# Odd layer of a hybrid encoder: conv-tile transposes issued two tiles later, SSD factors issued one head pair earlier

## The chip, the cores and the metric

The kernel runs on one core of a Trainium2 chip. A core has a matrix engine (TensorE, PE in the profile; PEld is its weight load), a vector engine (VectorE, DVE), an activation engine (ScalarE, ACT), a general engine (GpSimd, POOL) and a queue that starts transfers (SyncE, SP). Each engine runs its own list of instructions in order and waits on semaphores for the others. The metric is the device time of one execution in microseconds.

## The reference

A bidirectional encoder trunk with a sequence of 512, a width of 1024 and two layers, in float32. The first (even) layer is attention beside a convolution module. The second (odd) layer, which the change touches, projects the normalized input to 6192 columns and feeds two mixers from them:

```
u = rms_norm(x, norm_g) @ w_in
z_c, xbc, dt_f, dt_b, g_b, g_c, h_d, z_d = split(u)
xbc = silu(dw_conv5(xbc) + conv_b)          # x: 1536 columns, B: 4 x 128, C: 4 x 128
y   = ssd_scan forward + ssd_scan backward + d_skip * x      # 24 heads of 64, 4 groups, chunks of 128
o_c = group_rms_norm(y * silu(z_c))
o_d = g_b * dw_conv3(g_c * h_d) * silu(z_d)
x   = x + concat(o_c, o_d) @ w_out
```

Inside a chunk the scan is a product with a masked, decayed matrix; between chunks a state of 128 x 64 per head is carried. The program ends with an rms norm.

## The kernel before, in words

All large products are done with operands split into a high and a low part (fp32r), three matmuls for each pair of blocks: high by high, high by low, low by high. Weights arrive by DMA as slabs of 128 x 1024 (`w_raw`, two buffers); ScalarE makes the high part (L87) and, in the odd layer's input projection, POOL the low part (L88). `Weights.next` prepares one slab ahead of the one in use.

The odd layer's input projection is cut into 40 entries (`odd_tiles`): four z entries that are token-major, and 36 channel tiles of 128 channels by 512 positions. A channel tile is 24 matmuls of 512 columns into one of three `acc` banks (`mm_cm`, L318). Tiles of kind C, B and x go through `conv5` (L707 to L716): ScalarE writes the centre tap into an SBUF page, VectorE adds four taps from the bank (L714), ScalarE takes a tanh (L715), VectorE completes the silu (L716). B and x tiles are then turned on TensorE with four 128 x 128 transposes into an `sb` bank (helper `transposed`, L266) and copied by ScalarE. Tiles h, gc, gb and zd of each of four channel blocks make the short convolution.

The SSD works on four groups of six heads. `ssd_prepare(g)` makes the masked products of C and B (`cbm`) and the six states that enter the chunks: VectorE scales x (L854), TensorE multiplies by the turned B (L856), ScalarE or POOL and VectorE carry the state on (L859 to L862). `ssd_pairs(g)` treats three pairs of heads. For each head it makes the factor f of 128 x 512: VectorE and ScalarE alternate over the four chunks (L892, L893 on f; L897, L898 on the decay e, which `decays` fetches by DMA two heads ahead into a ring of four buffers), then an exponential (L900) and a product (L901). Then come eight matmuls with f (L904, into the only `cv` bank), the skip term (L913), the part of the states (L920 on TensorE, L925 and L928 on VectorE) and the gate product on POOL (L930). After each pair, `fill` issues a few tiles of the rest of the list. `ssd_finish(g)` takes the group norm and turns the result (L944, L266 into `tp`), scaled into the pages that the output projection reads.

The order of the code sets priorities and the buffers' order. The framework plans each engine's list from it ahead of time and may put an instruction whose inputs it takes to be late behind later ones: in the trace the transposes of a tile stand within the matmuls of the following tile. On the chip each list is then fixed.

`fill` issues in group order 5, 9, 9 and 8 tiles, in threes or twos after a pair; before the first group nine entries are issued (z, and group 0's C, B and three x tiles).

Of the kernel before, what the change touches and what calls it, by code (L numbers as in the profile page):

```python
# [159 lines left out]
def odd_tiles():  # L160

    group = lambda g: [("C", g), ("B", g), ("x", 3 * g), ("x", 3 * g + 1), ("x", 3 * g + 2)]
    short = lambda i: [("h", i), ("gc", i), ("gb", i), ("zd", i)]
    z = [("z", g) for g in range(4)]
    return z + group(0) + group(1) + short(0) + group(2) + short(1) + group(3) + short(2) + short(3)


ODD_TILES = odd_tiles()
# [2 lines left out]
def trunk(ctx, tc, A, out, dbg=None):  # L171
# [29 lines left out]
    def bank(tag):  # L201
        return ps.tile([P, S], F32, name=tag, tag=tag, bufs=banks[tag])
# [504 lines left out]
    def conv5(key, i, c):  # L707

        z = mm_cm(key, xT)
        w = lambda j: pc[:, PC["conv_c_w"][0] + i * 5 + j:PC["conv_c_w"][0] + i * 5 + j + 1]  # L710
        d = tmp("c5t", "c5", 3)
        SC.activation(c, z, AF.Identity, scale=w(2), bias=pcs("conv_c_b", i))  # L712
        for j, o, ii in taps5:
            V.scalar_tensor_tensor(c[:, o], z[:, ii], w(j), c[:, o], op0=ALU.mult, op1=ALU.add)  # L714
        SC.activation(d, c, AF.Tanh, scale=0.5)  # L715
        V.scalar_tensor_tensor(c, d, 1.0, c, op0=ALU.add, op1=ALU.mult)  # L716
# [9 lines left out]
    def channel_tile(kind, i):  # L726
# [6 lines left out]
        elif kind == "C":  # L733
            inp[i]["C"] = tmp("CT", "CT", 2)
            conv5("C", 16 + i, inp[i]["C"])
            inp[i]["x"] = tmp("xs", "xs", 2, (P, NT, GW))
        elif kind == "B":
            bt = tmp("BT", "BT", 1)
            conv5("B", 12 + i, bt)
            tp = transposed([bt[:, t * P:(t + 1) * P] for t in range(NT)], "sb")  # L740
            inp[i]["B"], inp[i]["Bt"] = bt, tmp("Bt", "Bt", 1)
            SC.copy(inp[i]["Bt"], tp)
        elif kind == "x":
            c = tmp("c5", "c5", 3)
            conv5("x", i, c)
            tp = transposed([c[:, t * P:(t + 1) * P] for t in range(NT)], "sb")
            g, j = divmod(i, 3)
            SC.copy(inp[g]["x"][:, :, j * P:(j + 1) * P], c4(tp))
        elif kind == "h":
            sc["h"] = tmp("sc_h", "c5", 3)  # L750
            SC.copy(sc["h"], mm_cm("h", xT))
        elif kind == "gc":
            z, hp = mm_cm("gc", xT), sc["h"]
            V.tensor_tensor(hp, z, hp, op=ALU.mult)
            c = oF[i] = page("oF", "keep")
            SC.activation(c, hp, AF.Copy, scale=cdw[:, i, 1:2])
            for j, o, ii in taps3:
                V.scalar_tensor_tensor(c[:, o], hp[:, ii], cdw[:, i, j:j + 1], c[:, o], op0=ALU.mult, op1=ALU.add)  # L758
        elif kind == "gb":
            z = mm_cm("gb", xT)  # L760
            V.tensor_tensor(oF[i], z, oF[i], op=ALU.mult)
        else:
            z = mm_cm("zd", xT)
            gate(sc["h"], z)
            G.tensor_tensor(oF[i], oF[i], sc["h"], op=ALU.mult)

    todo = iter(ODD_TILES)

    def fill(n):
        for _ in range(n):  # L770
            kind_i = next(todo, None)
            if kind_i:
                channel_tile(*kind_i)

    fill(2)

# [19 lines left out]
    back = bank("tp")  # L796
    for d in range(2):
        tp = transposed([d1[:, t, d * SH:(d + 1) * SH] for t in range(NT)], "tp", SH)
        cs = tmp("cs", "c5", 3)[:SH]
        for c in range(NT):  # L800
            o, i, z = cs[:, c * P:(c + 1) * P], tp[:, c * P:(c + 1) * P], ident[:SH]
            if d:
# [70 lines left out]
            nc.sync.dma_start(e, src.broadcast_to([P, 2, S]))  # L873
            ahead.append(e)

    def ssd_pairs(g, cbm, St, fills):

        CT, xs = inp[g]["C"], inp[g]["x"]
        hs = heads(g)
        for j in range(3):  # L880
            pr = slice(j * P, (j + 1) * P)
            yd = bank("cv")
            for i in range(2):
                hh = g * HPG + 2 * j + i
                hf, hb = hh, SH + hh

                decays(hh + 2)
                rb = ahead[hh]
                e, f = rb[:, 0], tmp("f", "f", 3)
                for c in range(NT):  # L890
                    cc = slice(c * P, (c + 1) * P)
                    SC.activation(f[:, cc], cbm[0][:, cc], AF.Copy, scale=dt[:, c, hf:hf + 1])  # L892
# [6 lines left out]
                                           op0=ALU.add, op1=ALU.min)  # L899
                SC.activation(e, e, AF.Exp)  # L900
                V.tensor_tensor(f, e, f, op=ALU.mult)  # L901
                for c in range(NT):
                    o = c * P + i * HD
                    T.matmul(yd[:, o:o + HD], f[:, c * P:(c + 1) * P],  # L904
# [23 lines left out]
                V.tensor_tensor(yc, yc, yw.rearrange("p (c d) -> p c d", c=3), op=ALU.add)  # L928
            zj = zg[g][:, :, pr]
            G.tensor_tensor(yt, yt, zj, op=ALU.mult)  # L930
            fill(fills[j])

    def ssd_finish(g):

# [7 lines left out]
        rsqrt(rs, ss, 4)  # L942
        for c in range(NT):
            V.tensor_scalar(xs[:, c], xs[:, c], rs[:, c:c + 1], None, op0=ALU.mult)  # L944
        for j in range(3):
            i = 3 * g + j
            tp = transposed([xs[:, c, j * P:(j + 1) * P] for c in range(NT)])
# [1 line left out]
                oF[4 + i] = zg[g].rearrange("p c d -> p (c d)")[:, j * S:(j + 1) * S]  # L949
                SC.activation(oF[4 + i], tp, AF.Copy, scale=pcs("ssd_norm", i))  # L950
            else:
                hi, lo = tmp("o_hi", *(("c5", 3), ("c5", 3), ("CT", 2))[j], dt=F32R), \
                    tmp("o_lo", *(("c5", 3), ("BT", 1), ("CT", 2))[j], dt=F32R)
                split_psum(hi, lo, tp, pcs("ssd_norm", i))
                last.append((hi, lo))

    last = []
    fill(7)
    pre = ssd_prepare(0)
    for g in range(GRP):  # L960
        ssd_pairs(g, *pre, ((2, 2, 1), (3, 3, 3), (3, 3, 3), (3, 3, 2))[g])
        if g < GRP - 1:
            pre = ssd_prepare(g + 1)
        ssd_finish(g)


    free = []
# [118 lines left out]
```

## Time and profile before

| | us |
|---|---|
| median of 3 runs | 1000.29 |
| lowest, highest | 997.64, 1002.73 |
| the profiled execution | 1003.47 |
| its span, first to last instruction | 1001.7 |

The granted clock of TensorE is the share of full speed that the hardware allowed; its mean over the profiled execution is 0.978. The odd layer's first z matmul starts at 509 us, its first channel tile ends at 590 us, the last channel tile ends at about 901 us, and the output projection runs from there to the end. In the views below a row of a group gives line, engine, operation, output and inputs, shapes and count, then busy time and mean length, then the engine's idle time just before and what ended it; a row of the timeline gives start, length, engine, line, operation and, in brackets, the idle time before and who ended it; a row of the waits gives who waited for whom, total us, times and the longest.

### The profile page before, as it was taken

The page shows a single profiled execution, that of the slowest core. Times are in us where ns is not written, and L with a number is a line of the kernel's source. Part 1 is how long each engine was busy: PE and PEld are TensorE (multiplying, and loading weights), DVE is VectorE, ACT ScalarE, POOL GpSimd, SP SyncE. Part 2 cuts the span into 40 slices and gives each one's busy share as a digit, 9 for nine tenths or more (in the row PEclk, how much of TensorE's full clock was granted, in tenths as well). Part 3 has the DMA queues.
Part 4 walks back from the last instruction along what each step waited for, and adds up shares of the span by engine and source line. Part 5 has one row for each costly group of instructions (what it writes and reads, how often), then busy time and mean ns, then how long its engine had stood idle before and what let it go on. Part 6 is the DMA issues. An engine that isn't in the chain of part 4 may idle for free. (4 is left out here: it accounts for less than half of the span.)

```text
span 1001.7 us, 12583 instructions
## 1 busy us (share of the span) xinstructions
PE 931.6 (93%) x4564; PEld 757.0 (76%) x4564; DVE 735.9 (73%) x1295; ACT 464.5 (46%) x916; POOL 384.0 (38%) x272
## 2 busy tenths in 40 slices
PE   7899999999999999699999999888869988999996
PEld 7887686686786777578889987676756876787885
DVE  4799989899898998922167537888998968956215
ACT  6646444454445453723143546456455555443312
POOL 0251743625428153531234354424433433445221
PEclk9999999999999999989999999989999998999999
DMA  8313322112213235033253533332333423322222
GB/s 302 101 29 111 55 68 70 49 40 84 69 25 115 74 31 170 22 127 105 81 173 92 168 125 96 95 110 83 92 120 84 122 90 102 109 101 82 92 84 84
DMA packets 42326, 95.99 MB, mean 96 GB/s; under 512 B 12136, under 2 KB 13800, under 8 KB 42264
## 3 DMA queue, kind: packets, MB, share of 16 engines
q1 hardware_dynamic: 42264, 95.19, 31.2%
q8 instruction: 36, 0.59, 0.2%
q14 instruction: 26, 0.21, 0.1%
HBM read 90.85 MB, written 4.33 MB: 95 GB/s over the span
## 5 line engine op out<-in xcount | busy, mean ns | idle before, releaser
L88 POOL TENSOR_TENSOR w_lo<-w_raw,w_hi 128x1024 fp32r<-128x1024 f32 (+2 forms) x68 | 159.5, 2347 | 267.2 <-ACT w_hi L87 181.2
L87 ACT CAST w_hi<-w_raw 128x1024 fp32r<-128x1024 f32 (+7 forms) x142 | 135.1, 952 | 221.8 <-PE acc L318 67.1
L318 PE MATMUL acc<-xT_hi,w_hi 128*128 128x512 f32 x544 | 222.0, 409 | 2.7 <-ACT xT_hi L404 2.7
L318 PE MATMUL acc<-xT_lo,w_hi 128*128 128x512 f32 x544 | 220.4, 406 | 0.4 <-POOL xT_lo L405 0.4
L88 DVE TENSOR_TENSOR w_lo<-w_raw,w_hi 128x1024 fp32r<-128x1024 f32 (+6 forms) x74 | 85.3, 1153 | 116.1 <-ACT w_hi L87 111.8
L318 PE MATMUL acc<-xT_hi,w_lo 128*128 128x512 f32 x544 | 142.7, 396 | 0.0
L479 DVE SCALAR_TENSOR_TENSOR cv<-u,pc,cv 128x497 f32<-128x497 f32 (+10 forms) x176 | 130.2, 740 | 10.0 <-ACT cv L468 7.7
L318 PEld LDWEIGHTS acc<-xT_hi,w_hi 128*128 128x128 f32 x544 | 105.3, 194 | 25.5 <-ACT xT_hi L404 2.9
L318 PEld LDWEIGHTS acc<-xT_lo,w_hi 128*128 128x128 f32 x544 | 105.3, 194 | 22.5 <-POOL xT_lo L405 0.8
L318 PEld LDWEIGHTS acc<-xT_hi,w_lo 128*128 128x128 f32 x544 | 101.9, 189 | 20.8
L477 POOL TENSOR_TENSOR side<-side 128x510 f32<-128x510 f32 (+3 forms) x56 | 77.9, 1391 | 4.7
L482 POOL TENSOR_TENSOR u<-cs,side 128x512 f32<-128x512 f32 x8 | 11.0, 1372 | 157.1 <-issue 149.9
L898 DVE SCALAR_TENSOR_TENSOR e<-e,nacs 128x128 f32<-128x128 f32 x96 | 50.8, 571 | 7.1 <-ACT e L897 7.1
L531 ACT ACTIVATE p<-sb,mx 128x512 f32<-128x512 f32 x64 | 43.4, 683 | 20.9 <-DVE mx L529 20.6
L476 POOL TENSOR_SCALAR side<-u,pc 128x510 f32<-128x510 f32 (+3 forms) x56 | 50.9, 910 | 4.7
L529 DVE TENSOR_REDUCE mx<-sb 128x1 f32<-128x512 f32 x64 | 41.7, 685 | 3.3 <-PE sb L527 2.6
L893 DVE SCALAR_TENSOR_TENSOR f<-cbm,dt,f 128x128 f32<-128x128 f32 x96 | 42.5, 488 | 0.4 <-ACT f L892 0.4
L897 ACT ACTIVATE e<-e,nacs 128x128 f32<-128x128 f32 x96 | 31.3, 391 | 21.6 <-DMA e<-acs 21.6
L266 PEld LDWEIGHTS tp<-kc,p 128*128 128x128 f32 x256 | 28.9, 140 | 16.0 <-ACT pt L554 10.7
L714 DVE SCALAR_TENSOR_TENSOR c<-acc,pc,c 128x510 f32<-128x510 f32 (+1 forms) x48 | 35.7, 744 | 6.7 <-ACT c L712 6.4
L527 PE MATMUL sb<-k_t,qk_hi 128*128 128x512 f32 (+1 forms) x128 | 39.5, 403 | 0.4 <-DVE k_t L257 0.3
L564 PE MATMUL acc<-pt,v_tm 128*64 128x512 f32 x128 | 37.6, 608 | 1.4 <-DVE pt L554 1.4
(336 smaller groups left out, 1927.4 us busy)
## 6 DMA issues: line engine op xcount, KB each, us to landing
w_raw<-in_w_cm_o SPq DMA_DIRECT2D x36, 512.0 KB, 3.5
w_raw<-in_w_cm_e SPq DMA_DIRECT2D x32, 512.0 KB, 3.5
e<-acs SPq DMA_DIRECT2D x24, 512.0 KB, 5.2
w_raw<-in_w_out_e SPq DMA_DIRECT2D x16, 512.0 KB, 3.5
w_raw<-in_w_out_o SPq DMA_DIRECT2D x16, 512.0 KB, 3.5
w_raw<-in_w_z SPq DMA_DIRECT2D x12, 384.0 KB, 3.2
xt<-in_xT SPq DMA_DIRECT2D x8, 256.0 KB, 5.4
x_t<-in_x SPq DMA_DIRECT2D x4, 512.0 KB, 6.5
```

What stands on the lines that cost most here:

```text
L87: nc.scalar.copy(hi, raw)
L88: eng.tensor_tensor(lo, raw, hi.bitcast(F32), op=ALU.subtract)
L318: T.matmul(a, l, r, start=n == 0, stop=n == 3 * kk - 1)
L476: G.tensor_scalar(t[:, o], ut[:, i], wt(j), 0.0, op0=ALU.mult, op1=ALU.add)
L477: G.tensor_tensor(side[:, o], side[:, o], t[:, o], op=ALU.add)
L479: V.scalar_tensor_tensor(c[:, o], ut[:, i], wt(j), c[:, o], op0=ALU.mult, op1=ALU.add)
L527: T.matmul(s, l[:, qs], r, start=n == 0, stop=n == 2)
L529: V.tensor_reduce(mx, s, axis=AX.X, op=ALU.max, negate=True)
L531: SC.activation(p, s, AF.Exp, bias=mx, accum_out=sums[:, q:q + 1])
L564: T.matmul(o[j * HD:(j + 1) * HD], v_tm[:, k, (h0 + j) * HD:(h0 + j + 1) * HD], pt, start=k == 0, stop=k == NT - 1, skip_group_check=True)
L893: V.scalar_tensor_tensor(f[:, cc], cbm[1][:, cc], dt[:, c, hb:hb + 1], f[:, cc], op0=ALU.mult, op1=ALU.add)
L898: V.scalar_tensor_tensor(e[:, cc], rb[:, 1, cc], nacs[:, c, hb:hb + 1], e[:, cc], op0=ALU.add, op1=ALU.min)
```

## The change

Four edits that go together. First, the turning of a B or x tile becomes a closure that `fill` calls once two further tiles have been issued (`late=2`); `fill(0)` calls all that are left. Second, `ssd_pairs` is split into `ssd_factors` (the two factors f of a pair) and `ssd_pair` (all that reads them); the factors of the next pair are issued before the matmuls of the current one. Third, in a group's last round `ssd_prepare` of the next group and its first factors are issued before the last pair, and the transposes of a finished group (`ssd_turn`) are issued after the next group's first fill. Fourth, the list of tiles spreads the short-conv tiles as 3, 3 and 10 behind groups 1, 2 and 3 and the fills become 8, 8, 8 and 7 tiles per group, each ahead of its pair. The tag `c5` has five buffers in place of three, `f` four in place of three. The buffer `xs` of a group is asked for at its first turn and no longer at its C tile.

```diff
@@ odd_tiles
-    return z + group(0) + group(1) + short(0) + group(2) + short(1) + group(3) + short(2) + short(3)
+    sh = [k for i in range(4) for k in short(i)]
+    return z + group(0) + group(1) + sh[:3] + group(2) + sh[3:6] + group(3) + sh[6:]
@@ conv5
-        d = tmp("c5t", "c5", 3)
+        d = tmp("c5t", "c5", 5)
@@ channel_tile
             conv5("C", 16 + i, inp[i]["C"])
-            inp[i]["x"] = tmp("xs", "xs", 2, (P, NT, GW))
         elif kind == "B":
             bt = tmp("BT", "BT", 1)
             conv5("B", 12 + i, bt)
-            tp = transposed([bt[:, t * P:(t + 1) * P] for t in range(NT)], "sb")
-            inp[i]["B"], inp[i]["Bt"] = bt, tmp("Bt", "Bt", 1)
-            SC.copy(inp[i]["Bt"], tp)
+
+            def turn():
+                tp = transposed([bt[:, t * P:(t + 1) * P] for t in range(NT)], "sb")
+                inp[i]["B"], inp[i]["Bt"] = bt, tmp("Bt", "Bt", 1)
+                SC.copy(inp[i]["Bt"], tp)
+            turns.append((nth[0], turn))
         elif kind == "x":
-            c = tmp("c5", "c5", 3)
+            c = tmp("c5", "c5", 5)
             conv5("x", i, c)
-            tp = transposed([c[:, t * P:(t + 1) * P] for t in range(NT)], "sb")
-            g, j = divmod(i, 3)
-            SC.copy(inp[g]["x"][:, :, j * P:(j + 1) * P], c4(tp))
+
+            def turn():
+                g, j = divmod(i, 3)
+                if j == 0:
+                    inp[g]["x"] = tmp("xs", "xs", 2, (P, NT, GW))
+                tp = transposed([c[:, t * P:(t + 1) * P] for t in range(NT)], "sb")
+                SC.copy(inp[g]["x"][:, :, j * P:(j + 1) * P], c4(tp))
+            turns.append((nth[0], turn))
@@ fill
-    def fill(n):
+    turns, nth = [], [0]
+
+    def fill(n, late=2):
+
         for _ in range(n):
             kind_i = next(todo, None)
             if kind_i:
                 channel_tile(*kind_i)
+            nth[0] += 1
+            while turns and turns[0][0] < nth[0] - late:
+                turns.pop(0)[1]()
+        if not n:
+            while turns:
+                turns.pop(0)[1]()
@@ ssd_pairs
-    def ssd_pairs(g, cbm, St, fills):
...
+    def ssd_factors(g, j, cbm):
+
+        fs = []
+        for i in range(2):
                 hh = g * HPG + 2 * j + i
...
                 decays(hh + 2)
                 rb = ahead[hh]
-                e, f = rb[:, 0], tmp("f", "f", 3)
+                e, f = rb[:, 0], tmp("f", "f", 4)
...
                 V.tensor_tensor(f, e, f, op=ALU.mult)
+                fs.append(f)
+        return fs
+
+    def ssd_pair(g, j, fs, St):
...
+            yd = bank("cv")
+            for i, f in enumerate(fs):
                 for c in range(NT):
                     o = c * P + i * HD
                     T.matmul(yd[:, o:o + HD], f[:, c * P:(c + 1) * P],
...
             G.tensor_tensor(yt, yt, zj, op=ALU.mult)
-            fill(fills[j])
@@ ssd_finish
             V.tensor_scalar(xs[:, c], xs[:, c], rs[:, c:c + 1], None, op0=ALU.mult)
+        return lambda: ssd_turn(g, xs)
+
+    def ssd_turn(g, xs):
         for j in range(3):
...
     fill(7)
-    pre = ssd_prepare(0)
+    fill(0)
+    cbm, St = ssd_prepare(0)
+    fs = ssd_factors(0, 0, cbm)
+    finish = None
     for g in range(GRP):
-        ssd_pairs(g, *pre, ((2, 2, 1), (3, 3, 3), (3, 3, 3), (3, 3, 2))[g])
-        if g < GRP - 1:
-            pre = ssd_prepare(g + 1)
-        ssd_finish(g)
+        for j in range(3):
+            fill(((3, 3, 2), (3, 3, 2), (3, 3, 2), (3, 2, 2))[g][j])
+            if finish:
+                finish()
+                finish = None
+            if j < 2:
+                nxt = ssd_factors(g, j + 1, cbm), St
+            elif g < GRP - 1:
+                fill(0)
+                cbm, nst = ssd_prepare(g + 1)
+                nxt = ssd_factors(g + 1, 0, cbm), nst
+            ssd_pair(g, j, fs, St)
+            fs, St = nxt
+        finish = ssd_finish(g)
+    finish()
```

More of the change, by code (lines that the diff above doesn't have):

```diff
@@ L739, in channel_tile @@
             conv5("B", 12 + i, bt)
-            tp = transposed([bt[:, t * P:(t + 1) * P] for t in range(NT)], "sb")
-            inp[i]["B"], inp[i]["Bt"] = bt, tmp("Bt", "Bt", 1)
-            SC.copy(inp[i]["Bt"], tp)
+            def turn():
[3 more added lines that the diff above has]
+            turns.append((nth[0], turn))
         elif kind == "x":
-            c = tmp("c5", "c5", 3)
+            c = tmp("c5", "c5", 5)
             conv5("x", i, c)
-            tp = transposed([c[:, t * P:(t + 1) * P] for t in range(NT)], "sb")
-            g, j = divmod(i, 3)
-            SC.copy(inp[g]["x"][:, :, j * P:(j + 1) * P], c4(tp))
+            def turn():
[5 more added lines that the diff above has]
+            turns.append((nth[0], turn))
         elif kind == "h":
-            sc["h"] = tmp("sc_h", "c5", 3)
+            sc["h"] = tmp("sc_h", "c5", 5)
             SC.copy(sc["h"], mm_cm("h", xT))
@@ L798, in trunk @@
         tp = transposed([d1[:, t, d * SH:(d + 1) * SH] for t in range(NT)], "tp", SH)
-        cs = tmp("cs", "c5", 3)[:SH]
+        cs = tmp("cs", "c5", 5)[:SH]
         for c in range(NT):
@@ L874, in decays @@
             ahead.append(e)
-    def ssd_pairs(g, cbm, St, fills):
[L878 to L883, printed above, removed]
+    def ssd_factors(g, j, cbm):
+        fs = []
+        for i in range(2):
                 hh = g * HPG + 2 * j + i
@@ L901, in ssd_pairs @@
                 V.tensor_tensor(f, e, f, op=ALU.mult)
+                fs.append(f)
+        return fs
+    def ssd_pair(g, j, fs, St):
+        CT, xs = inp[g]["C"], inp[g]["x"]
+        hs = heads(g)
+        if True:
+            pr = slice(j * P, (j + 1) * P)
+            yd = bank("cv")
+            for i, f in enumerate(fs):
                 for c in range(NT):
@@ L951, in ssd_finish @@
             else:
-                hi, lo = tmp("o_hi", *(("c5", 3), ("c5", 3), ("CT", 2))[j], dt=F32R), \
-                    tmp("o_lo", *(("c5", 3), ("BT", 1), ("CT", 2))[j], dt=F32R)
+                hi, lo = tmp("o_hi", *(("c5", 5), ("c5", 5), ("CT", 2))[j], dt=F32R), \
+                    tmp("o_lo", *(("c5", 5), ("BT", 1), ("CT", 2))[j], dt=F32R)
                 split_psum(hi, lo, tp, pcs("ssd_norm", i))
```

## The prediction

> **What bounds the kernel now.** I read the page's busy row first, then the busy times by stretch, then what TensorE waited for.
>
> ```profile
> span 1001.7 us, 12583 instructions
> PE 931.6 (93%) x4564; PEld 757.0 (76%) x4564; DVE 735.9 (73%) x1295; ACT 464.5 (46%) x916; POOL 384.0 (38%) x272
> ```
>
> TensorE (PE) is busy 93% of the span, so the whole kernel is TensorE's; a change of order can win only what TensorE loses: its idle time and the time at a lower clock. The stretches say where that is (columns: stretch, length, busy us of PE, PEld, DVE, ACT and POOL, each with its instructions, granted clock, DMA share, GB/s).
>
> ```profile
> 690.00:757.00 67.00, 53.72 (x272) 44.69 (x271) 61.91 (x125) 33.85 (x72) 24.31 (x13) 0.95 0.34 97
> ...
> 837.00:890.00 53.00, 50.96 (x257) 41.30 (x257) 41.54 (x75) 24.29 (x53) 22.70 (x13) 0.95 0.34 111
> 610.00:890.00 280.00, 245.93 (x1221) 198.91 (x1220) 241.49 (x459) 146.29 (x325) 110.07 (x61) 0.96 0.34 102
> 890.00:910.00 20.00, 18.23 (x78) 14.69 (x78) 15.18 (x32) 11.78 (x25) 7.65 (x5) 0.91 0.16 54
> ```
>
> The stage of the change is 610 to 890 us: TensorE idles 280 - 245.9 = 34.1 us, and a clock of 0.96 costs at most 0.04 x 280 = 11 us more. In the same stretch VectorE (DVE) is busy 241.5 us, nearly as long as TensorE. So two engines share the stage almost evenly: TensorE cannot be relieved by more than VectorE can follow. In the last part (837 to 890, few conv tiles left) TensorE is already dense.
>
> What TensorE waited for from 610 to 910 us (total, times, longest):
>
> ```profile
> PE sb L266 <- DVE c L716: 11.6, 4, 4.4
> PE cv L904 <- DVE f L901: 9.4, 6, 2.6
> PE sb L266 <- DVE BT L716: 6.7, 2, 3.4
> PE tp L266 <- DVE xs L944: 4.2, 2, 2.4
> PE tp L266 <- DVE St L862: 1.4, 3, 0.5
> PE tp L856 <- DVE St L862: 1.2, 3, 0.5
> PE tp L856 <- DVE gt L854: 1.1, 1, 1.1
> ```
>
> All are waits for VectorE, together 35.6 us (one of 1.77 us lies behind 890). There is none for weights and none for a free accumulator. Transposes of conv tiles (c and BT, L266 into sb) make 18.3, the matmuls with a head's factor f (L904) 9.4, the transposes of a finished group 5.6, the states (L856) 2.3.
>
> How one such wait looks, in TensorE's order of time:
>
> ```profile
> 655.05 0.40 PE L318 MATMUL acc<-xT_lo,w_hi 128*128 128x512 f32 x1
> 658.68 1.12 PE L266 MATMUL sb<-kc,c 128*128 128x128 f32 x4 [3.24 <-DVE c L716]
> ...
> 660.03 0.63 PE L318 MATMUL acc<-xT_lo,w_hi 128*128 128x512 f32 x1
> 660.45 0.63 PE L318 MATMUL acc<-xT_hi,w_hi 128*128 128x512 f32 x1
> ```
>
> Two matmuls into the next tile TensorE meets the transposes of the tile before, 3.24 us too early, with the rest of the ready matmuls queued behind. After the gap matmuls start 0.42 us apart (660.03, 660.45): that is the clock loss. The order was fixed beforehand, and VectorE ran late against it.
>
> **The change, part by part.** It adds and removes no arithmetic and no transfer: 31 tiles, 64 conv transposes, 24 heads, 12 pairs, four finishes stay. It changes order, and gives the tag c5 two buffers more and f one more.
>
> *Transposes two tiles later (18.3 us of waits).* Length of a tile, and VectorE's chain behind one, from an undisturbed place:
>
> ```profile
> 590.41 0.39 PE L318 MATMUL acc<-xT_hi,w_hi 128*128 128x512 f32 x1
> ...
> 595.85 0.39 PE L318 MATMUL acc<-xT_hi,w_hi 128*128 128x512 f32 x1
> ...
> 602.08 0.66 PE L266 MATMUL sb<-kc,BT 128*128 128x128 f32 x4
> ```
> ```profile
> 596.86 3.11 DVE L714 SCALAR_TENSOR_TENSOR BT<-acc,pc,BT 128x510 f32<-128x510 f32 x4 [0.28 <-ACT BT L712]
> 600.68 0.62 ACT L715 ACTIVATE c5t<-BT 128x512 f32<-128x512 f32 x1
> 601.33 0.69 DVE L716 SCALAR_TENSOR_TENSOR BT<-c5t,BT 128x512 f32<-128x512 f32 x1 [1.36 <-ACT c5t L715]
> ```
>
> A tile takes 595.85 - 590.41 = 5.44 us of TensorE. B's accumulation started at 590.41, and its last matmul was followed by the next tile at 595.85; VectorE ended at 602.02, 6.2 us later. Two tiles give 10.9 us: 4.7 us more than the bare chain. The longest wait now is 4.4 us past a place that already lies inside the next tile. So I expect these waits gone one by one: gain between 0 (they turn into another wait, below) and 18.3 us plus up to 11 us of clock. TensorE needs a free one of three acc banks for the next tile, and a bank is free when VectorE has done its four taps; that wait does not occur in this trace, so its price lies between 0 and the whole 18.3.
>
> *Factors a pair ahead (9.4 us).* A pair's L904 matmuls now follow a whole fill of two or three tiles (10.9 to 16.3 us) behind their factors. Gain 0 to 9.4. The e transfers are issued with the factors, up to a pair earlier on SP's queue, behind the weights of the fill:
>
> ```profile
> e<-acs SPq DMA_DIRECT2D x24, 512.0 KB, 5.2
> ```
>
> A fill of at least 10.9 us covers the 5.2 of landing, so I count nothing; without the cover a pair would pay up to 5.2 on ScalarE. On POOL the weight subtractions of a fill now stand ahead of the pair's gate product (L930) rather than behind it; weights are made a tile ahead and TensorE waits for none, so nothing, and if that cover goes a subtraction costs its length, about 2.4 us (the row of 721.04 below). The fourth f holds two pairs of two.
>
> *Finish, next group's states.* The transposes of a finished group (5.6 us with the St waits) come after the next fill: 0 to 5.6. The states' serial chain keeps its form: its 2.3 us stay.
>
> *Tiles per group* go from 5, 9, 9, 8 to 8, 8, 8, 7: no cost, and a more even load on both engines. A short-conv page waits in c5 over five conv tiles; three x pages, one c5t and this page fill the five buffers exactly, which I count at nothing since the next page is asked for only after the oldest was transposed.
>
> *An added wait:* C of group g+1 is written into the buffer of C of g-1, whose last reader (L920 of the last pair) now stands directly ahead. It is in order on TensorE, so 0; if C's matmuls are put ahead of it, ScalarE holds C's first activation and every cast and factor behind it, at most one tile each, 3 x 5.4 = 16 us. I take 0, since the emitted order has it so.
>
> *What is late next: VectorE.* Removing TensorE's waits helps until VectorE has no idle time left. Its waits from 610 to 890:
>
> ```profile
> DVE c L716 <- ACT c5t L715: 6.5, 5, 2.0
> DVE sc_h L754 <- PE acc L318: 6.2, 1, 6.2
> DVE St L862 <- POOL St L861: 6.1, 10, 0.7
> DVE c L714 <- ACT c L712: 3.9, 4, 2.8
> DVE f L901 <- ACT e L900: 3.3, 2, 3.1
> DVE xs L913 <- PE cv L904: 2.8, 3, 1.4
> DVE CT L716 <- ACT c5t L715: 2.4, 3, 1.0
> DVE CT L714 <- ACT CT L712: 2.3, 1, 2.3
> DVE gt L854 <- PE tp L856: 1.3, 2, 0.7
> ```
>
> With 2.5 us of small ones they are 37.3 of the 38.5 us that VectorE idles. Those behind an accumulator that came late (6.2 + 3.9 + 2.3 + 2.8 = 15.2) should go, as TensorE no longer stalls ahead of them. Those inside a chain of two engines stay: tanh 6.5 + 2.4, states 6.1, half of the other 7.1, together 18.5. So the stage lasts 241.5 + 18.5 = 260 us, 20 less than 280; TensorE then needs 235 to 246 of the 260. The 3.5 us lost from 890 to 910 (1.77 idle, 1.8 of clock) I leave as they are, the rest too. **Sum:** the profiled execution took 1003.47 us (span 1001.7 and 1.8 around it); less 20 is 983.5. The median of the three runs, 1000.29, lies 3.2 below the profiled one, so on its scale: 980.
>
> **A rule against it.** VectorE's busy time is partly waiting:
>
> ```profile
> 709.33 1.13 DVE L898 SCALAR_TENSOR_TENSOR e<-e,nacs 128x128 f32<-128x128 f32 x4
> ...
> 720.61 3.01 DVE L898 SCALAR_TENSOR_TENSOR e<-e,nacs 128x128 f32<-128x128 f32 x3
> 721.04 2.43 POOL L88 TENSOR_TENSOR w_lo<-w_raw,w_hi 128x1024 fp32r<-128x1024 f32 x1 [1.81 <-ACT w_hi L87]
> ```
> ```profile
> L893 DVE SCALAR_TENSOR_TENSOR f<-cbm,dt,f 128x128 f32<-128x128 f32 x96 | 42.5, 488 | 0.4 <-ACT f L892 0.4
> L898 DVE SCALAR_TENSOR_TENSOR e<-e,nacs 128x128 f32<-128x128 f32 x80 | 42.5, 571 | 1.1 <-ACT e L897 1.1
> L901 DVE TENSOR_TENSOR f<-e,f 128x512 f32<-128x512 f32 x24 | 19.4, 810 | 3.3 <-ACT e L900 3.3
> ```
>
> Four L898 take 1.13 us alone (0.28 each), three take 3.01 beside a subtraction on POOL that ends with them. At 0.28 each the 96 L893 would be 27 instead of 42.5 and the 80 L898 22.6 instead of 42.5: 35 us of stretch in these two lines alone, I estimate 50 with the rest. [...]
>
> **Rivals.**
> 1. *VectorE stretched by POOL: slower.* The stage has 110.1 us of POOL work, of which some 50 now block VectorE; the rest falls on VectorE's idle time or its reads of PSUM. If factors, issued in a block, meet POOL more often, VectorE grows. My stage breaks even at 20 us more stretch; at the far end all POOL work blocks, 60 us more, and the stage takes 320, or +40. At two thirds of that, 40 us more, it takes 300, or +20: 1020. Against it: POOL's instructions are the same in number and length. [...]
> 2. *The waits only change their name: the same.* TensorE stalls at L318 for a bank that VectorE has not emptied, or the order laid out beforehand puts ready work ahead as it does now (the transposes already stand inside a later tile). VectorE's share stays at 86 to 88%: 0 to -6, about 997.
> 3. *TensorE alone bounds.* VectorE's stretch shrinks and all 34.1 us and most of the 11 us of clock are won, about -44 in all: 956.
>
> **How the numbers follow.** Forecast (968 to 992): 0.55. Rival 2 (992 to 1004): 0.21. Rival 1 (over 1005): 0.12. Rival 3 (under 965): 0.12. About 0.5%, 5 us, is what a measurement of this kernel can tell from no change, so faster means under 995.3: 0.55 + 0.12 + a third of 0.21 = 0.74; same 0.14; slower 0.12. The range leaves out the lower half of rival 3 (0.07) and rival 1 (0.12): 960 to 1004.
>
> **What would show it.** Right: the waits of sb L266 for c and BT and of cv L904 for f nearly gone, clock near 1.00, VectorE over 92% in the stage, and TensorE's remaining waits, some 15 to 25 us, at acc L318 for L714. Rival 1: L893 and L898 well over 0.5 us each. Rival 2: VectorE's share unchanged, and as much wait under other names. Rival 3: VectorE's busy time in the stage far under 241. I am wrong if ScalarE, held by a buffer, starves VectorE: then VectorE's waits for L712, L897 or L900 grow.

## The result and the profile after

The changed kernel takes 1013.69 us (median of four runs, 1010.41 to 1014.84) against 1000.92 us (997.64 to 1002.73) for the kernel before on the same chip. The ratio is 1.0121 with a 95% interval of 1.0096 to 1.0145: 1.2% slower, where 980 us was forecast, and outside the range of 960 to 1004.

The profiled run took 1014.84 us. First the head of its page and the same two stretches as before (columns as there), then two stretches of 5 us that follow each other:

```profile
span 1013.0 us, 12565 instructions
PE 939.7 (93%) x4564; PEld 767.8 (76%) x4564; DVE 750.2 (74%) x1295; ACT 461.9 (46%) x916; POOL 382.2 (38%) x272
```
```profile
610.00:890.00 280.00, 247.98 (x1178) 204.06 (x1176) 245.88 (x447) 144.15 (x326) 105.86 (x59) 0.91 0.34 102
...
790.00:795.00 5.00, 0.39 (x2) 0.42 (x3) 5.00 (x11) 0.00 (x0) 2.06 (x1) 0.76 0.59 191
795.00:800.00 5.00, 5.00 (x27) 5.00 (x26) 2.11 (x7) 3.15 (x6) 0.00 (x0) 0.50 0.15 58
```

The span grew by 1013.0 - 1001.7 = 11.3 us. TensorE runs the same 4564 matmuls, but they take 8.1 us longer (939.7 against 931.6), and its idle time rose by the other 3.2 us. The granted clock of the stage fell from 0.96 to 0.91. The two short stretches show how: after a long stall (790 to 795, TensorE busy 0.39 us) the next 5 us run at a clock of 0.50. Here a slow stretch follows the stall, so the wait is paid for twice. Added up from stretches of 1 us between 610 and 950, TensorE runs some 58 us at half clock in the changed kernel and 27 us in the kernel before: eight falls of the clock against seven, most of them longer.

What TensorE waited for (total, times, longest), and the three places that matter most in its timeline:

```profile
PE tp L267 <- DVE xs L966: 19.6, 4, 7.9
PE tp L872 <- DVE cbm L862: 8.4, 2, 4.6
PE sb L267 <- DVE c L717: 4.0, 1, 4.0
PE tp L872 <- ACT St L875: 3.2, 1, 3.2
PE tp L872 <- DVE gt L870: 3.1, 3, 2.0
PE tp L872 <- DVE St L878: 1.0, 2, 0.5
PE tp L943 <- DVE St L878: 0.5, 1, 0.5
```
```profile
688.94 1.62 PE L872 MATMUL tp<-gt,Bt 128*128 128x384 f32 x2 [4.56 <-DVE cbm L862]
...
794.61 1.51 PE L267 MATMUL tp<-kc,xs 128*128 128x128 f32 x6 [6.35 <-DVE xs L966]
...
924.67 1.51 PE L267 MATMUL tp<-kc,xs 128*128 128x128 f32 x6 [7.87 <-DVE xs L966]
```

The waits that the change is aimed at are gone or small: the conv tiles' transposes (sb L267) fell from 18.3 to 4.0 us, the matmuls with f from 9.4 to nothing. In their place TensorE waits for a finished group's normalized xs (19.6, before 4.2) and for the next group's masked products and states (8.4 + 3.2 + 3.1 + 1.0). All seven sum to 39.8 us, against 35.6 before. They are fewer and longer: 39.8 us in 14 waits, 35.6 us in 21 before. No wait stands at an accumulator.

Apart from one wait of 3.2 us for ScalarE, VectorE is still what they wait for, and it became busier by 14.3 us (750.2 against 735.9) with the same 1295 instructions. The groups of its factor steps f and e, and of the scaled x of the states, then the one row of before that the prediction did not show:

```profile
L905 DVE SCALAR_TENSOR_TENSOR f<-cbm,dt,f 128x128 f32<-128x128 f32 x96 | 59.3, 658 | 0.0
L910 DVE SCALAR_TENSOR_TENSOR e<-e,nacs 128x128 f32<-128x128 f32 x80 | 36.3, 486 | 0.8 <-ACT e L909 0.8
L870 DVE TENSOR_TENSOR gt<-xs,d 128x384 f32<-128x384 f32 x24 | 21.4, 932 | 2.6 <-ACT xs L755 2.6
```
```profile
L854 DVE TENSOR_TENSOR gt<-xs,d 128x384 f32<-128x384 f32 x24 | 11.9, 548 | 1.4 <-PE tp L856 1.3
```

Against 488 ns an f step now takes 658, the scaled x 932 against 548; e became shorter (486 against 571). POOL's work did not grow (382.2 us against 384.0): it met other VectorE steps. One such meeting, in the timeline of the changed kernel:

```profile
651.25 2.44 POOL L88 TENSOR_TENSOR w_lo<-w_raw,w_hi 128x1024 fp32r<-128x1024 f32 x1 [10.56 <-ACT w_hi L87]
651.35 6.20 DVE L905 SCALAR_TENSOR_TENSOR f<-cbm,dt,f 128x128 f32<-128x128 f32 x3
653.66 1.35 POOL L953 TENSOR_TENSOR xs<-xs,zg 128x512 f32<-128x512 f32 x1
654.96 2.44 POOL L88 TENSOR_TENSOR w_lo<-w_raw,w_hi 128x1024 fp32r<-128x1024 f32 x1
...
785.12 0.16 DVE L240 TENSOR_TENSOR rs_t<-rs_y 128x4 f32<-128x4 f32 x1
785.43 2.40 POOL L88 TENSOR_TENSOR w_lo<-w_raw,w_hi 128x1024 fp32r<-128x1024 f32 x1 [4.06 <-ACT w_hi L87]
785.46 2.39 DVE L241 TENSOR_TENSOR rs_t<-rs_t,ss 128x4 f32<-128x4 f32 x1
...
789.63 2.43 POOL L88 TENSOR_TENSOR w_lo<-w_raw,w_hi 128x1024 fp32r<-128x1024 f32 x1 [1.80 <-ACT w_hi L87]
789.77 2.31 DVE L240 TENSOR_TENSOR rs_t<-rs_w 128x4 f32<-128x4 f32 x1
```

Three f steps last 6.20 us, as long as the three POOL operations in a row beside them (651.25 to 657.40). And of the tiny steps of the group norm, 128x4 and 0.16 us long, two are held for 2.39 and 2.31 us by a subtraction each: some 4.4 us of delay in the chain for which TensorE then waits 6.35 us at 794.61.

**Theories for the experiments.** T1: the lock between POOL's subtractions and VectorE is the price (the prediction's rival 1). T2: the order costs by itself: at the tail, where nothing covers the last group's norm, at the group boundary, or through the tiles ahead of the pairs. T3: late transposes or factors ahead are harmful themselves.

### The profile page after: what moved, and what is told of

Same layout as the page of the kernel before. It is cut to its first block, busy times and chain, and to the rows that moved or that the text cites. A ratio compares the mean times of both kernels' runs of the same rounds, so it can differ in the third digit from the quotient of the medians.

```text
span 1013.0 us, 12565 instructions
## 1 busy us (share of the span) xinstructions
PE 939.7 (93%) x4564; PEld 767.8 (76%) x4564; DVE 750.2 (74%) x1295; ACT 461.9 (46%) x916; POOL 382.2 (38%) x272
## 5 line engine op out<-in xcount | busy, mean ns | idle before, releaser
L319 PE MATMUL acc<-xT_lo,w_hi 128*128 128x512 f32 x544 | 216.7, 399 | 0.0
L319 PE MATMUL acc<-xT_hi,w_lo 128*128 128x512 f32 x544 | 137.0, 390 | 0.0
L905 DVE SCALAR_TENSOR_TENSOR f<-cbm,dt,f 128x128 f32<-128x128 f32 x96 | 59.3, 658 | 0.0
L910 DVE SCALAR_TENSOR_TENSOR e<-e,nacs 128x128 f32<-128x128 f32 x96 | 44.6, 500 | 6.8 <-ACT e L909 6.8
L267 PEld LDWEIGHTS tp<-kc,p 128*128 128x128 f32 x256 | 29.6, 143 | 15.9 <-ACT pt L555 9.9
L872 PE MATMUL tp<-gt,Bt 128*128 128x384 f32 x48 | 24.5, 614 | 15.7 <-DVE cbm L862 8.4
## 6 DMA issues: line engine op xcount, KB each, us to landing
w_raw<-in_w_z SPq DMA_DIRECT2D x12, 384.0 KB, 3.3
```

The costliest lines, as they stand in the source:

```text
L267: T.transpose(tp[:rows, j * P:(j + 1) * P], b, ident)
L319: T.matmul(a, l, r, start=n == 0, stop=n == 3 * kk - 1)
L905: V.scalar_tensor_tensor(f[:, cc], cbm[1][:, cc], dt[:, c, hb:hb + 1], f[:, cc], op0=ALU.mult, op1=ALU.add)
L910: V.scalar_tensor_tensor(e[:, cc], rb[:, 1, cc], nacs[:, c, hb:hb + 1], e[:, cc], op0=ALU.add, op1=ALU.min)
```

## The experiments

All were timed beside runs of the kernel before on the same chip; ratios are to those.

**The tail.** The list ends in the changed kernel before the last pair; in the kernel before, two tiles stood behind it. e1 puts two back.

```diff
-            fill(((3, 3, 2), (3, 3, 2), (3, 3, 2), (3, 2, 2))[g][j])
+            end = g == GRP - 1 and j == 2
+            if not end:
+                fill(((3, 3, 2), (3, 3, 2), (3, 3, 2), (3, 2, 2))[g][j])
...
         finish = ssd_finish(g)
+    fill(2)
     finish()
```

> The changed kernel with its last fill of two tiles put back behind the last pair, ahead of the last group's transposes. Theory of order: the last group's finish has lost the two tiles (10.9 us of TensorE) that covered it before; TensorE's wait for xs near the end falls from 7.9 us to under 2 and the matmuls at half clock behind it go, so 8 to 10 us less than the changed kernel, about 1004. Theory of the lock (VectorE stretched by POOL sets the pace): VectorE ends its last group at the same time, the two tiles only fill a wait, and the gain is the same or smaller, 3 to 8 us; the rest of the stage does not move in either.

Measured: 1006.72 us, ratio 1.0045 (1.0022 to 1.0067), 7.0 us less than the change. The wait of 7.87 us at 925 is gone (three waits for xs, 11.7 us, in place of four, 19.6); f steps stay at 658 ns. So the tail is worth 7 us, and the rest of the loss lies elsewhere. The 7.0 us lie in the range forecast for the lock and just under that for order, so this run does not tell the two apart.

**The finish one fill later**, `if finish and j == 1:` in place of `if finish:`.

> The changed kernel with the transposes of a finished group issued after the second fill of the next group instead of the first (groups 0 to 2; the last group as in the change). Theory of order: the three waits for xs inside the stage (3.1, 6.4 and 2.3 us) and the half clock behind them go, 10 to 15 us less, about 1000. Theory of the lock: VectorE keeps its pace, the waits turn up at other lines, and the time moves by less than 4 us.

Measured: 1005.65 us, ratio 1.0048 (1.0026 to 1.0070). Its waits, where they differ:

```profile
PE sb L267 <- DVE c L717: 11.1, 4, 4.2
PE tp L267 <- ACT zg L975: 9.8, 2, 5.2
PE tp L267 <- DVE xs L966: 7.9, 1, 7.9
```

Of the waits for xs only that of the tail is left, but the c waits are back and two new ones appear, for ScalarE's copy of the turned group. Eight us are won, between the two forecasts. In the profiled execution (1003.37 us) TensorE is busy 929.6 us in place of 939.7; its waits have moved rather than gone: 38.4 us in 17 waits, against 39.8 in 14.

**Without POOL's subtractions.** In e3 (the changed kernel) and e4 (the kernel before) the low parts of the odd input projection's weights are left out: ScalarE copies the raw slab into the low buffer, so 52 operations leave POOL and none reaches VectorE. e11 is e3 with e1's tail.

```diff
-        eng.tensor_tensor(lo, raw, hi.bitcast(F32), op=ALU.subtract)
+        if eng is nc.gpsimd and key not in ("oe", "oo"):
+            nc.scalar.copy(lo, raw)
+        else:
+            eng.tensor_tensor(lo, raw, hi.bitcast(F32), op=ALU.subtract)
```

> The changed kernel, where the low parts of the odd layer's input weights are not computed: ScalarE copies the raw slab into that tile, so POOL has 52 subtractions less and ScalarE 52 copies of about 1 us more. Theory of the lock: the factor product on VectorE falls from 658 to about 300 ns, VectorE's busy time by 45 to 60 us, and the time by 25 to 45 us, to about 980. Theory of order: VectorE gets shorter but TensorE still meets the group transposes and states too early; under 15 us less, about 1000.

> The kernel before with the same omission (the low parts of the odd layer's input weights are copies made by ScalarE). Theory of the lock: the kernel before is held by VectorE less than the changed one, so it gains less, 10 to 25 us, about 983, and the order of the two kernels turns round: the changed one becomes the faster. Theory of order: both gain alike and the changed kernel stays about 10 us slower.

> The changed kernel with the mended tail, and the low parts of the odd layer's input weights left out as before (copies by ScalarE in their place). With the lock out of the way the pipeline should show what it is worth: the only long wait left was the one of 7.9 us near the end, so 5 to 8 us less than the same omission without the mended tail, about 960, and below the kernel before with the omission, 966.7. If the changed order wins nothing even then, it stays within 2 us of 967.

Measured: e3 967.16 us (0.9655, 0.9635 to 0.9675), e4 966.69 (0.965, 0.963 to 0.967), e11 959.48 (0.9599, 0.9573 to 0.9625). The busy rows of the pages of e3 and e4:

```profile
PE 919.1 (95%) x4564; PEld 749.5 (78%) x4564; DVE 692.6 (72%) x1295; ACT 506.4 (52%) x968; POOL 264.1 (27%) x220
```
```profile
PE 921.0 (95%) x4564; PEld 750.0 (78%) x4564; DVE 694.1 (72%) x1295; ACT 508.8 (53%) x968; POOL 262.5 (27%) x220
```

VectorE's busy time falls by 750.2 - 692.6 = 57.6 us in the changed kernel and by 735.9 - 694.1 = 41.8 in the one before, with VectorE's own instructions unchanged. So 58 and 42 us of what looked like VectorE's work was time spent beside POOL, and the whole increase of 14 us that the change brings is of this kind. The times fall by 47 and 34 us and become equal. Neither theory had forecast that: by the lock the change was to become the faster, by order it was to stay 10 us behind. The f step falls to 456 ns (e3) and 399 (e4), not to the 300 forecast; what holds it above that is not shown. With the tail mended as well the change is then 5 to 7 us ahead (e11 against e4, by the ratios and by the medians): its idea works once VectorE keeps up.

T1 holds for the net loss, which goes with the subtractions. It does not hold for the tail: the wait of 7.9 us for the last xs stands in e3 too, and mending it wins 6 to 8 us there (e11 against e3). That price is one of order.

**The same subtractions, cut or moved.** e5 (before) and e6 (change with e1's tail) cut each POOL subtraction in four; e7 (before), e8 (change with e1's tail) and e12 (change as it is) give the odd input projection's subtractions to VectorE.

```diff
-        eng.tensor_tensor(lo, raw, hi.bitcast(F32), op=ALU.subtract)
+        q = kt * n // 4 if eng is nc.gpsimd else kt * n
+        for o in range(0, kt * n, q):
+            eng.tensor_tensor(lo[:, o:o + q], raw[:, o:o + q], hi[:, o:o + q].bitcast(F32), op=ALU.subtract)
```
```diff
-        eng = nc.vector if key in EARLY or key in ("oe", "oo") and self.i % 2 else nc.gpsimd
+        eng = nc.vector if key not in ("oe", "oo") or key in ("oe", "oo") and self.i % 2 else nc.gpsimd
```

> The kernel before, each weight subtraction on POOL cut into four of a quarter of the columns; nothing is left out. If VectorE and POOL exclude each other for a whole instruction, VectorE is held for at most a quarter of 2.4 us at a time: its mean e and f steps fall from 571 and 488 ns towards 400, and the time by 8 to 20 us, about 986. If they share bandwidth and the stretch is a matter of amount, or if order alone decides, the stretch stays and the time moves by less than 4 us, or grows by POOL's 100 or so more instructions.

> The changed kernel with its tail mended (as in the first experiment) and the subtractions on POOL cut into four. Exclusion for a whole instruction: f steps fall from 658 ns towards 450, VectorE's waits get short, and the time falls from about 1006 by 15 to 25 us, to about 985; the change then costs nothing or wins a little. Sharing by amount: within 4 us of 1006.

> The kernel before with the low parts of the odd layer's input weights made by VectorE and not by POOL; nothing is left out. In the stage VectorE gets 31 subtractions of 1.15 us, 36 us, and loses the stretch by them, which was 15 to 20 in e and f and some 30 to 35 in all. Theory of the lock: about even on VectorE, but the long unplanned holds go, so the time falls by 3 to 15 us, about 991. Theory of order: VectorE has no less to do and the time does not fall.

> The changed kernel with the mended tail and these low parts on VectorE. Theory of the lock: its stretch was larger by some 15 us, so it gains 10 to 25 us on the mended kernel and ends at about 988, beside or below the kernel before with the same edit. Theory of order: within 4 us of 1006.

> The change as it is, tail not mended, with the low parts of the odd layer's input weights on VectorE; nothing is left out. If the tail costs about 6 us whatever the rest does, this takes about 982, 6 more than with the mended tail and about as long as the kernel before with the same edit (984.3). If the tail only costs where VectorE is late by POOL, it takes within 2 us of 975.4.

Measured: e5 993.82 us (0.9934, 0.9916 to 0.9953), e6 990.09 (0.9896, 0.9864 to 0.9929), e7 984.33 (0.9849, 0.9815 to 0.9883), e8 975.43 (0.9757, 0.9718 to 0.9796), e12 973.99 (0.9753, 0.9717 to 0.9788). The busy row of e7's page, and the longest wait of e12:

```profile
PE 928.2 (94%) x4564; PEld 755.1 (77%) x4564; DVE 751.2 (76%) x1347; ACT 465.6 (47%) x916; POOL 263.1 (27%) x220
```
```profile
PE acc L344 <- DVE w_lo L88: 6.5, 1, 6.5
```

Cut in four (e5), the kernel before gains 0.66%. Its f and e steps fall only to 473 and 522 ns, where some 400 was forecast, but VectorE's busy time falls by 13.9 us (722.0 against 735.9) although POOL's grows from 384.0 to 423.4: how long POOL holds VectorE at a time counts, not only how much POOL does. The change with its tail mended gains 1.5% by the same cut (e6 against e1; f steps 540 ns) and is then not told apart from e5, since the intervals overlap.

In e7 VectorE does 52 subtractions more, some 67 us of work, and its busy time grows by only 15.3 us (751.2 against 735.9), because its own steps are held less (f 401 ns, e 356). On this footing the change wins: e8 and e12 lie 9 to 10 us under e7, and 2.5% under the kernel before. The tail's edit is then worth nothing (e12 has one long wait of 6.5 us at the head of the output projection, e8 one of 5.8 for the last xs).

**One part of the change undone.** e9 turns tiles at once (`late=0`); e10 issues the factors right before their pair; e14 does both.

```diff
-    def fill(n, late=2):
+    def fill(n, late=0):
```
```diff
-    fs = ssd_factors(0, 0, cbm)
...
+            fs = ssd_factors(g, j, cbm)
+            nst = St
-            if j < 2:
-                nxt = ssd_factors(g, j + 1, cbm), St
-            elif g < GRP - 1:
+            if j == 2 and g < GRP - 1:
                 fill(0)
                 cbm, nst = ssd_prepare(g + 1)
-                nxt = ssd_factors(g + 1, 0, cbm), nst
             ssd_pair(g, j, fs, St)
-            fs, St = nxt
+            St = nst
```

> The changed kernel with one part undone: the transposes of a B or x tile follow their own tile again (late=0); fills, factors and finish stay changed. If the late transposes do what they were meant to and another part of the change costs the time, TensorE's waits at sb for c and BT come back, 10 to 18 us, and the time grows by 3 to 12 us, to about 1020. If VectorE's pace alone sets the stage, these waits only take the place of others and the time stays within 4 us of 1013.

> The changed kernel with one part undone: the factors of a pair are issued right ahead of that pair, after the fill, and no longer a pair ahead; the next group's states still come ahead of the last pair. If the block of factors issued ahead is what meets POOL's subtractions, the mean of an f step falls from 658 ns to 480 to 540, waits at cv for f come back, 6 to 12 us, and the time is 3 to 10 us less, about 1007. If the stretch has nothing to do with where the factors are issued, f stays over 620 ns and the time grows by the waits, to about 1020.

> The changed kernel with the transposes at once and the factors right before their pair: only the new list (tiles ahead of pairs) and the boundary are left of the change. If the late transposes and the factors ahead each lengthen the factor steps alone, so that undoing one showed nothing, L905 falls to 490 to 550 ns here and the time comes to 1000 to 1006. If neither does, L905 stays at 630 to 670 and the time at 1011 to 1017.

Measured: e9 1014.21 us (1.0144, 1.0118 to 1.0171), e10 1011.54 (1.0122, 1.0098 to 1.0145), e14 1012.27 (1.0109, 1.0075 to 1.0142); f steps 666, 647 and 653 ns. The waits of e9:

```profile
PE tp L267 <- DVE xs L966: 19.5, 4, 7.9
PE sb L267 <- DVE c L717: 12.0, 4, 4.1
PE tp L872 <- DVE St L878: 3.4, 7, 1.0
PE sb L267 <- DVE BT L717: 2.4, 1, 2.4
PE tp L872 <- DVE gt L870: 1.7, 1, 1.7
PE tp L943 <- DVE St L878: 0.9, 3, 0.5
```

The c and BT waits come back with 14.4 us, those for cbm and for ScalarE's St go, and the sum is 39.9 us, as in the changed kernel (39.8). TensorE waits as long as before, only under other names. T3 falls: neither part harms, and neither helps here. In e10 the f steps stay long, as one of its forecasts had it, but no wait for f comes back and the time does not grow: it was not the factors ahead that removed that wait.

**One part alone.** e15 is the kernel before with the new list only: 8, 8, 8 and 7 tiles, each fill ahead of its pair, `c5` of five. e16 is the kernel before with late transposes only.

```diff
-    return z + group(0) + group(1) + short(0) + group(2) + short(1) + group(3) + short(2) + short(3)
+    sh = [k for i in range(4) for k in short(i)]
+    return z + group(0) + group(1) + sh[:3] + group(2) + sh[3:6] + group(3) + sh[6:]
...
+            fill(fills[j])
             yd = bank("cv")
...
-            fill(fills[j])
...
-        ssd_pairs(g, *pre, ((2, 2, 1), (3, 3, 3), (3, 3, 3), (3, 3, 2))[g])
+        ssd_pairs(g, *pre, ((3, 3, 2), (3, 3, 2), (3, 3, 2), (3, 2, 2))[g])
```

> The kernel before with only the new list: fills of 8, 8, 8 and 7 tiles, each ahead of its pair, and c5 of five buffers; transposes at once, factors at their pair, boundary as before. If the list carries the price, L893 rises from 488 to 600 ns or more and the time to 1008 to 1016. If it does not, L893 stays at 470 to 520 and only the tail shows (the last two tiles no longer behind the last pair, about 7 us by e1): 1003 to 1009, with the long wait at the last group's transposes.

> The kernel before with only the late transposes (two tiles behind their own) and c5 of five buffers. By the prediction's first step the waits for c and BT (18.3 us) go nearly all: 985 to 992 if nothing takes their place. If VectorE, with its factor steps stretched by POOL, sets the pace, the time stays within 4 us of 1000.5, and other waits (for f at its matmuls, states, a finished group) grow by 10 us or more in sum. L893 over 550 ns here would show the late transposes as a source of the stretch.

Measured: e15 1010.89 us (1.0093, 1.0058 to 1.0127), e16 1004.67 (1.0034, 1.0018 to 1.0051). The two largest waits of e15; then the largest of e16, and two places of it in e16's timeline:

```profile
PE tp L267 <- DVE xs L945: 17.9, 4, 7.9
PE sb L267 <- DVE c L717: 13.7, 5, 5.0
```
```profile
PE sb L266 <- DVE c L716: 22.0, 5, 6.9
```
```profile
750.06 1.12 PE L266 MATMUL sb<-kc,c 128*128 128x128 f32 x4 [5.84 <-DVE c L716]
...
754.93 1.12 PE L266 MATMUL sb<-kc,c 128*128 128x128 f32 x4 [3.33 <-DVE c L716]
```

The list alone brings the long waits for xs, the tail's 7.9 us among them, and removes those for f: none at cv is left. Its f steps take 573 ns, between the two values forecast. Of its 0.93% the tail explains 0.76 (e1); what is left is less than the interval. Late transposes alone leave the f steps short (445 ns), so they are no source of the stretch, and make the c waits longer (22.0 us, before 11.6): in the old list a group's last x tiles stand right ahead of its states, which need them, so `fill(0)` turns them there together, and TensorE waits for one after the other (5.84 and 3.33 us). That the new list, with short-conv tiles behind a group's x tiles, is what gives the delay its room is read from the code and these places; it was not tried by itself.

**The group boundary.** e13 puts the next group's products, states and first factors behind the last pair again and turns a finished group at once; e17 adds two tiles behind the last pair, e18 also gives the subtractions to VectorE.

```diff
-            if finish:
-                finish()
-                finish = None
...
-            elif g < GRP - 1:
-                fill(0)
-                cbm, nst = ssd_prepare(g + 1)
-                nxt = ssd_factors(g + 1, 0, cbm), nst
             ssd_pair(g, j, fs, St)
             fs, St = nxt
-        finish = ssd_finish(g)
-    finish()
+        if g < GRP - 1:
+            fill(0)
+            cbm, St = ssd_prepare(g + 1)
+            fs = ssd_factors(g + 1, 0, cbm)
+        ssd_finish(g)()
```

> The changed kernel with the group boundary as before: the next group's products, states and first factors come after the last pair of the group, and a finished group's transposes at once. Late transposes, factors ahead within a group and the new list stay. If the boundary is what lays VectorE's factor steps beside POOL's subtractions, L905 falls from 658 ns to 550 or less and the time to 1003 or less (ratio at most 1.003). If it is the list, L905 stays at 640 to 670 and the time within 4 us of 1013.7, apart from the tail: the last group's finish is as in the changed kernel, so the wait for the normalized group of 7.9 us at 925 us stays in both cases.

> The changed kernel with the group boundary as before and the last two tiles behind the last pair; late transposes, factors ahead within a group and the rest of the list stay. If the list's price is the tail, this is e13 less some 7 us: the time 996 to 999.5, ratio to before 0.994 to 0.998, and no wait of 7.9 us for the last normalized group. If the list also costs in the steady part, 1001 to 1005 and ratio 1.000 to 1.004. VectorE's factor step L905 should be at 630 to 670 ns in both cases, which would say that the longer factor step alone does not make the change slow, since other VectorE steps became shorter.

> As e17, and the low parts of the odd input projection's weights are made by VectorE in place of POOL. If the boundary's price of 9 us is one of order by itself, this wins it over e8 (975.43): 964 to 969. If the boundary cost because VectorE was late beside POOL, nothing is left to win: 972 to 977, within 3 us of e8 and e12.

Measured: e13 1004.88 us (1.0039, 1.0024 to 1.0054), e17 997.54 (0.9963, 0.9941 to 0.9985), e18 975.30 (0.9746, 0.9723 to 0.9768). The head of e13's page, the busy row of e17's (span 994.9 us), then e17's two largest waits:

```profile
span 1005.1 us, 12569 instructions
PE 933.5 (93%) x4564; PEld 760.5 (76%) x4564; DVE 743.5 (74%) x1295; ACT 462.0 (46%) x916; POOL 383.2 (38%) x272
```
```profile
PE 929.9 (93%) x4564; PEld 757.3 (76%) x4564; DVE 743.1 (75%) x1295; ACT 462.0 (46%) x916; POOL 384.0 (39%) x272
```
```profile
PE tp L267 <- DVE xs L966: 15.0, 3, 5.1
PE tp L859 <- DVE gt L948: 5.2, 2, 2.7
```

Tail and boundary form a square, and the parts add: as the change is 1.0121; tail mended 1.0045; boundary undone 1.0039; both 0.9963. The tail costs 0.76% either way, the boundary 0.82%, and what is left of the change is a gain of 0.37%: in all, 7.6 + 8.2 - 3.7 = 12.1 us of 1000. Each ratio is known to some 0.2 points, so that they add to the last digit is partly luck; and e17 puts the two tiles ahead of the last group's norm, e1 behind it. The 7.9 us between the spans of the change and of e13 are 6.2 of TensorE's busy time (939.7 - 933.5), that is clock (44 us at half clock from 610 to 950 in place of 58), and 1.7 idle. f steps stay at 647 ns in e13 and 652 in e17: their length is not the price by itself, since with VectorE's sum at 743 us the kernel is no slower than before. And with the subtractions on VectorE the boundary costs nothing: e18 (975.30) equals e8 (975.43), which has the boundary of the change. So T2 is right on where; on why, T2 holds at the tail (e11 against e3) and T1 at the boundary: the block of products, states and factors ahead of the last pair costs only beside POOL. The tail's price was not seen with the subtractions on VectorE (e12 against e8), for which no run gives the reason.

That it is the block's place in VectorE's list that makes it late there was not tried by itself and stays argued.

## Why the prediction was wrong

- **The bound.** That TensorE and VectorE share the stage, and that TensorE can win no more than VectorE can follow, holds as far as it was tried: undoing single parts left the sum of TensorE's waits at 36.4 to 39.9 us (e9, e10, e14), and taking POOL's subtractions away brought it to 11.8 (e3).
- **The step that failed** is the sum, "the stage lasts 241.5 + 18.5 = 260 us". It took VectorE's busy time as fixed and let 20 us of its idle time go. For the same 1295 instructions over the whole kernel, VectorE's busy time grew by 14.3 us, all of it time beside POOL (without the subtractions e3 and e4 have 692.6 and 694.1), and its idle time fell by only 3.0 us, from 1001.7 - 735.9 = 265.8 to 1013.0 - 750.2 = 262.8. Together that is the span's growth of 11.3 us. Nor did the waits behind a late TensorE, 15.2 us of the 20, go: from 610 to 890 the changed kernel still has 12.9 us of them, 1.4 for a c page and these:

```profile
DVE xs L936 <- PE cv L927: 6.0, 2, 3.2
DVE sc_h L762 <- PE acc L319: 5.5, 1, 5.5
```

  VectorE's share of that stretch went from 86 to 88%, where over 92% was to show a success.
- **Rival 1, VectorE stretched by POOL**, names the mechanism behind the boundary's 0.82% and the net loss, and was given 0.12; the tail's 0.76% it did not have. "Against it: POOL's instructions are the same in number and length" was true (382.2 us) and no argument: the same 52 subtractions cost VectorE 42 us in the old order and 58 in the new (e4, e3). Its own price was not reached: VectorE grew by 14.3 us, under the 20 at which the prediction's stage breaks even, and the kernel lost all the same, since the 20 us of idle time that were to pay for it did not go. The estimate of 50 us of stretch in the kernel before was near: 41.8 in e4. VectorE's reads of PSUM it left out of the stretch, and at L714, which reads an `acc` bank, the traces agree: in the kernel before each of the 80 steps took 733 to 751 ns, also beside a subtraction (four in 3.10 us from 807.40, beside two that run from 806.77 to 811.50).
- **Transposes two tiles later:** the waits fell to 4.0 of 18.3 us as forecast, and the time won was 0 (e9), the lower end of the step. The fear for an accumulator was unfounded.
- **Factors a pair ahead:** the 9.4 us are gone, but through the tiles ahead of the pairs, which remove them alone (e15) and keep them away without the factors ahead (e10).
- **"Finish: 0 to 5.6" gained:** the waits for xs rose from 4.2 to 19.6 us instead, 7.9 of them in the tail. The list alone brings them (17.9 in e15), not the later transposes: with the finished group turned at once they are 22.8 (e13).
- **"The states' 2.3 us stay":** 15.7 us now (8.4 + 3.2 + 3.1 + 1.0), with the boundary moved.
- **"890 to 910, I leave as they are"** cost 7 us (e1, and e17 against e13). The last two tiles used to run while VectorE normalized the last group; the row in the kernel before is the wait of 1.77 us, in the changed kernel that of 7.87.

```profile
902.71 1.89 PE L266 MATMUL tp<-kc,xs 128*128 128x128 f32 x8 [1.77 <-DVE xs L944]
```

- **"Tiles per group: no cost"** is where this tail was overlooked: the list alone is 0.93% slower (e15).
- **The clock** was to come near 1.00; it fell to 0.91, with 58 us at half clock in place of 27. That fewer and longer waits are the reason is argued from the traces, not tried.
- **Rival 2, the waits only change their name**, at about 997, is what the change comes to without its tail and boundary (e17, 997.54: 30.6 us of waits in place of 35.6, most for xs and gt).

## What to carry to other kernels

Before moving work ahead of an engine that is nearly full, split that engine's busy time into its own work and the time it is held: instructions of one shape with two lengths, and another engine's instruction that starts and ends with the long ones, show it. Where such a lock exists, taking it away (here, the subtractions moved from POOL to VectorE: 1.5% alone, 2.5% with the change) comes before any reordering, since until then the waits mostly change their names. When a list of filler work is redistributed, ask at each place that loses its filler what covered the chain there, the last place above all.

## What the runs showed of the hardware

- A subtraction on POOL can hold VectorE for the whole of POOL's instruction even where VectorE's is tiny: 128x4 steps of 0.16 us took 2.31 and 2.39 us beside one (rows at 785 and 789 above).
- With POOL's operation cut in four VectorE is held less: in e5 its f and e steps take 473 and 522 ns, in the kernel before 488 and 571, and the product that ends a factor (f from e and f) 746 in place of 810. The main groups of the subtraction, before and in e5:

```profile
L88 POOL TENSOR_TENSOR w_lo<-w_raw,w_hi 128x1024 fp32r<-128x1024 f32 x44 | 108.9, 2476 | 164.2 <-ACT w_hi L87 78.2 <-PE acc L318 27.2 <-issue 19.2
```
```profile
L90 POOL TENSOR_TENSOR w_lo<-w_raw,w_hi 128x256 fp32r<-128x256 f32 x176 | 138.1, 815 | 141.5 <-ACT w_hi L87 58.1 <-PE acc L320 22.1 <-issue 21.1
```

  A slab costs POOL 4 x 815 = 3260 ns in place of 2476, and the kernel still gains 0.66% (e5).
- The granted clock can fall to half behind a stall of 2.26 us, and can stay full behind a longer one. The stall and the 5 us after it in the changed kernel, then one in the kernel before and its surroundings:

```profile
868.86 1.33 PE L267 MATMUL tp<-kc,xs 128*128 128x128 f32 x5 [2.26 <-DVE xs L966]
```
```profile
870.00:875.00 5.00, 4.94 (x29) 4.83 (x28) 1.34 (x3) 4.13 (x11) 3.60 (x2) 0.61 0.30 101
```
```profile
737.53 0.66 PE L266 MATMUL sb<-kc,BT 128*128 128x128 f32 x4 [3.32 <-DVE BT L716]
```
```profile
735.00:740.00 5.00, 2.47 (x13) 2.15 (x14) 5.00 (x9) 3.35 (x7) 1.92 (x2) 1.00 0.00 0
```

  Behind the 2.26 us the clock is 1.00 until about 871 and 0.50 from there to about 878, although TensorE is busy 4.94 of the 5 us. Behind the 3.32 us it stays at 1.00, here and on to 745. What follows differs: transposes and matmuls of 64 columns in the first place, matmuls of 512 columns soon in the second; whether that decides was not tried.
